# A fused block of four token mixers on one core: other buffer counts, priority bands and assumed latencies around two recurrences

## Chip, cores and metric

One NeuronCore of a Trainium2 chip runs the whole layer in one launch. The metric is the device time of that launch in microseconds; smaller is better. TensorE is called PE here (PEld is its weight load), VectorE DVE, ScalarE ACT, GpSimd POOL and SyncE SP.

## What is computed

For 512 tokens of width 2048 (one batch, float32) the layer normalises x, projects it with `w_in` into five groups, runs four mixers of 1024 channels each, gates the joined result with silu(z) and projects it back with `w_out`:

```python
h = rms_norm(x, norm_g[l])
p = jnp.einsum('bsd,dn->bsn', h, w_in[l])
p_rwkv, p_fox, p_gdn, p_diff, z = jnp.split(p, bounds, axis=-1)
y = jnp.concatenate([rwkv7_time_mix(p_rwkv, ...), forgetting_attention(p_fox, ...),
                     gated_deltanet(p_gdn, ...), differential_attention(p_diff, l, ...)], axis=-1)
x = x + jnp.einsum('bsm,md->bsd', y * jax.nn.silu(z), w_out[l])
```

Two mixers are recurrences over the tokens (`rwkv7_time_mix` with a state of 64 x 64 per head, `gated_deltanet` with 128 x 128 per head, after a causal convolution of 4 taps over its q, k and v); two are softmax attentions.

## The kernel before

Every projection is split into three float32r matmuls (high x high, low x high, high x low). A raw weight tile `wr` of 128 x 1024 comes by one or two DMAs from SP's queue; `wsplit` makes `wh` from it with a cast on ACT (L313) and `wl` with a subtraction on DVE (L314). `wr`, `wh` and `wl` are rings of buffers (`tag`, `bufs`).

`main()` is a stream of projections. After a prologue it runs eight steps `j`, each for one slice of 128 channels of all four mixers: r, k, v of rwkv (`acc_r`, `acc_k`, `acc_v`), then v, k, q of the delta net (`acc_gv`, `acc_gk`, `acc_gq`), then `acc_fqk`, `acc_vv`, `acc_dqk` of the attentions. Then come the z projections (`acc_z`) and the output projection (`acc_o`). The mixers run as threads (Python generators) beside the stream. In step `j` the two recurrences of slice `j-1` and the attention `diff` of `j-1` are still at work: `rwkv_chain` in eight chunks (`pC`), `gdn_chain` in four (`pG`). A chunk of `rwkv_chain` goes PE (`pC<-ZV,ET` and `pC<-Sb,AR`), ACT copy `rs` (L712), DVE addition `rs` (L717), ACT copy `yt` (L719), PE (`pC<-rs,ET`), DVE copy `ZV` (L725), PE (`pC<-ZV,...`), DVE update `Sb`. The chunk of a chain is written chunk c of chain j below.

The order on PE is fixed while the program is built: `pe[0]` adds up an assumed time of the matmuls written so far, a thread that yields a number is taken up again 1.25 times (`SLACK`) that many microseconds later, and between the two the stream writes matmuls. A thread or the stream that yields a name waits until that part has been written. So a yield is an assumed latency: too small a number makes PE meet an instruction whose input is late, too large a number makes a recurrence slow. The order on DVE, ACT, POOL and SP comes from a scheduler that takes priorities: `band(...)` sets them (`PRIO_CHAIN` first, then `PRIO_W`, `PRIO_EVAC`, `PRIO_MIX`, `PRIO_FILL`, `PRIO_GEMM`). On the chip each engine works through its queue strictly as built.

`gdn_evac` (L793) convolves a projection into `gc_v`, `gc_k` or `gc_q`. `gdn_local` applies silu to them, loads and prepares the decay tile `GA` (DMA L821, sixteen operations on POOL at L828, an exponential on ACT at L830), transposes and forms `pK`. `inverses` solves the triangular systems on DVE (`bP`, `bX`, L970) and multiplies their blocks on PE (`pmr`, `pmg`). `put_y` stores a finished slice to DRAM.

Of the kernel before, what the change touches and what calls it, by code (L numbers as in the profile page):

```python
# [20 lines left out]
P = 128  # L21
# [33 lines left out]
def hybrid_kernel(ctx: ExitStack, tc: tile.TileContext, ins, out, steps=tuple(range(NJ)), ydbg=None, tail=True):  # L55
# [71 lines left out]
    def until(*what):  # L127

        while what not in done:
            yield 0.5  # L130
# [85 lines left out]
    for part in range(4):  # L216
        if part == 2:
            load_x(1)
        wr = wp.tile([P, 1024], F32, name=f"w0r{part}", tag="wr", bufs=3) if part < 2 else \
            mp.tile([P, 1024], F32, name=f"w0r{part}")  # L220
        load_tm(wr, part, FOX0 + 2 * G, DIFF0 + 2 * G)
        w0.append((wr, mp.tile([P, 1024], F32R, name=f"w0h{part}"), mp.tile([P, 1024], F32R, name=f"w0l{part}")))
# [92 lines left out]
        return wh, wl  # L315

    def wtile():
        return wp.tile([P, WN], F32, name=f"wr{wcount[0]}", tag="wr", bufs=3)

    def gemm_fm(c0, name, then=None):  # L320
        acc = None
# [44 lines left out]
    ydr = [dr.tile([P, T], F32, name=f"ydr{m}") for m in range(MT)]  # L366

    def put_y(m, y):
        nc.sync.dma_start(ydr[m], y)
        if ydbg is not None:  # L370
            nc.sync.dma_start(ydbg[m], y)

# [321 lines left out]
    def rwkv_chain(j, st, XT):  # L694
# [7 lines left out]
        for c in range(NCH):  # L702
            AR, ET, BKt, ZV = (st[n][c // 4][:, c % 4] for n in ("AR", "ET", "BKt", "ZV"))
            yield from free("cr")
            ps = bank("cr", f"pC{j}_{c}", 1.0e9)

            for h in range(2):
                hs = slice(h * C, (h + 1) * C)
                MM(ps[0:R_, P + h * C:P + (h + 1) * C], ET[:, h, 0:R_], ZV[:, hs], start=True, stop=True)
            if c:  # L710
                MM(ps[:, 0:P], AR.rearrange("p a t -> p (a t)"), Sb, start=True, stop=True)
            nc.scalar.copy(rs[0:C], ps[0:C, P:2 * P])  # L712
            yield 2.4
            y = yt[(c % 2) * C:(c % 2 + 1) * C, c // 2, :]
            if c:
                band(PRIO_CHAIN)
                TT(rs[0:C], rs[0:C], ps[0:C, 0:P], op=ALU.add)  # L717
                band(PRIO_MIX)
                nc.scalar.copy(y, ps[C:P, 0:P])  # L719
            for h in range(2):  # L720
                hs = slice(h * C, (h + 1) * C)
                MM(ps[0:R_, 2 * P + h * C:2 * P + (h + 1) * C], ET[:, h, 0:R_], rs[:, hs], start=True, stop=True)
            yield 2.0
            band(PRIO_CHAIN)
            nc.vector.tensor_copy(ZV[0:C, :], ps[0:C, 2 * P:3 * P])  # L725
            band(PRIO_MIX)
            for h in range(2):
                hs = slice(h * C, (h + 1) * C)
                MM(ps[C:P, 3 * P + h * C:3 * P + (h + 1) * C], ET[:, h, R_:R_ + C], ZV[:, hs], start=True, stop=True)

            if c < NCH - 1:
                for h in range(2):
                    hs = slice(h * C, (h + 1) * C)
                    MM(ps[hs, P:P + C], BKt[:, h], ZV[:, hs], side=2, start=True, stop=True)
            pe[0] += 0.2
            if c < NCH - 1:
                band(PRIO_CHAIN)
                W = Wc[:, c:c + 1]
                tS = mp.tile([P, C], F32, name=f"tS{j}_{c}", tag="tS", bufs=1)
                for h in range(2):  # L740
                    hs = slice(h * C, (h + 1) * C)
                    if c:
                        TS(tS[hs, :], Sb[hs, hs], W[hs, :], None, op0=ALU.mult)
                for h in range(2):
                    hs = slice(h * C, (h + 1) * C)
                    o = ps[hs, P:P + C]
                    if c:
                        STT(Sb[hs, hs], o, W[hs, :], tS[hs, :], op0=ALU.mult, op1=ALU.add)
                    else:
                        TS(Sb[hs, hs], o, W[hs, :], None, op0=ALU.mult)  # L750
                band(PRIO_MIX)
            if c:
                TT(y, y, ps[C:P, 3 * P:4 * P], op=ALU.add)
            else:
                nc.scalar.copy(y, ps[C:P, 3 * P:4 * P])
            release(f"pC{j}_{c}", 3.0)
            if c % 4 == 3:
                done.add(("rwkv_half", j, c // 4))

# [24 lines left out]
    def gdn_evac(j, i, acc):  # L784
        s = "qkv"[i]
        n = 8 * i + j
        if s == "v":
            a = mp.tile([P, T], F32, name=f"gc_{s}{j}", tag="gc_v", bufs=1)
        else:
            a = mp.tile([P, T], F32, name=f"gc_{s}{j}", tag=f"gc_{s}", bufs=1)  # L790
        ACT(a, acc, AF.Copy, scale=convw(3, n))
        for d in (1, 2, 3):
            STT(a[:, d:T], acc[:, 0:T - d], convw(3 - d, n), a[:, d:T], op0=ALU.mult, op1=ALU.add)  # L793
        return a
# [19 lines left out]
        return pt  # L814

    def gdn_local(j, res):

        yield from until("gdn_chain", j - 1)
        GA = mp.tile([P, NT, 2, P], F32, name=f"GA{j}", tag="GA", bufs=1)
        Dm = GA[:, :, 1, :]  # L820
        nc.gpsimd.dma_start(Dm, gcd[:, j, :].unsqueeze(0).to_broadcast([P, NT, P]))  # L821
        gdn_silu(j, "v", res["v"])
        yield 2.5
        band(PRIO_FILL)
        for c in range(NT):
            for b in range(4):
# [5 lines left out]
                                fill=0.0, base=0, channel_multiplier=-1)  # L832
        band(PRIO_MIX)

        yield from until("gk", j)
        k2 = res["k"]
        gdn_silu(j, "k", k2)
        yield 7.0
        yield from free("tr")
        pt = gdn_transposed(j, "k", k2)  # L840
        KTs = mp.tile([P, NT, P], F32, name=f"KTs{j}", tag="KTs", bufs=1)
# [15 lines left out]
        vn = mp.tile([P, NT, P], F32, name=f"vn{j}", tag="vn", bufs=1)  # L857
        TT(vn, pt.rearrange("p (t f) -> p t f", f=P), vn_s.unsqueeze(2).to_broadcast([P, NT, P]), op=ALU.mult)

        yield from until("gq", j)  # L860
        q2 = res["q"]
        gdn_silu(j, "q", q2)
        yield 8.0
        for q in range(2):
            yield from free("sc")
            ps = psc(f"pK{j}_{q}", 2.5)
# [16 lines left out]
    def gdn_chain(j, st, XG):  # L883
# [3 lines left out]
        for c in range(NT):  # L887
# [3 lines left out]
            if c:  # L891
# [2 lines left out]
                rs = mp.tile([P, P], F32, name=f"grs{j}_{c}", tag="gs", bufs=4)  # L894
                band(PRIO_CHAIN)
                STT(rs, ps[:, 0:P], eg_neg[:, c, j:j + 1], vn[:, c, :], op0=ALU.mult, op1=ALU.add)
                band(PRIO_MIX)
                ACT(ot[:, c, :], ps[:, P:2 * P], AF.Copy, scale=eg[:, 0, c, j:j + 1])
            else:
                rs = vn[:, 0, :]  # L900
            yield 2.4
            MM(ps[:, 2 * P:3 * P], XG[:, c, :], rs, start=True, stop=True)
            Y = mp.tile([P, P], F32, name=f"gY{j}_{c}", tag="gs", bufs=4)
            band(PRIO_CHAIN)
            nc.scalar.copy(Y, ps[:, 2 * P:3 * P])
            band(PRIO_MIX)
            yield 2.4
            if c < NT - 1:
                MM(ps[:, 0:P], KTs[:, c, :], Y, start=True, stop=True)
            MM(ps[:, 3 * P:4 * P], GA[:, c, 1, :], Y, start=True, stop=True)  # L910
# [8 lines left out]
            else:  # L919
                TS(ot[:, c, :], ps[:, 3 * P:4 * P], -1.0, None, op0=ALU.mult)  # L920
            band(PRIO_MIX)
            release(f"pG{j}_{c}", 3.2)
        done.add(("gdn_chain", j))
        sq = mp.tile([P, T], F32, name=f"osq{j}", tag="tmp", bufs=2)
        ACT(sq, ot.rearrange("p t f -> p (t f)"), AF.Square)
# [23 lines left out]
    def inverses(j, ET, GA, blk, start_rwkv):  # L949
# [14 lines left out]
        nc.gpsimd.memset(Xf[64:112, 1:512:34], 1.0)  # L964
        pr = lcp.tile([112, 512], F32, name=f"bP{j}", tag="lc", bufs=8)
        for t in range(1, 32):
            band(PRIO_FILL)
            n, w = (t + 1) // 2, t + 1
            pv_ = pr[:, 0:n * w].rearrange("p (a b) -> p a b", b=w)
            TT(pv_, X[:, 0:n, 0:w], A[:, 0:w, t].unsqueeze(1).to_broadcast([112, n, w]), op=ALU.mult)  # L970
# [20 lines left out]
        XQ = mp.tile([P, 4, 32], F32, name=f"XQ{j}", tag="gs", bufs=4)  # L991
        for g in range(4):
            nc.gpsimd.dma_start(XQ[32 * g:32 * g + 32], xb[16 + g:32:4].rearrange("m s t -> s m t"))
        yield 14.5
        yield from until("rwkv_local", j)

        XN = lcp.tile([P, 16, 32], F32, name=f"XN{j}", tag="lc", bufs=8)
# [84 lines left out]
    def qk_heads(j, ev, kind):  # L1082
# [1 line left out]
        gi = 0 if kind == "fox" else 2  # L1084
        TS(ss, ss, 1.0 / C, 1e-6, op0=ALU.mult, op1=ALU.add)
        rs = rsqrt(mp, ss, 16, "qk", f"{kind}{j}")
        yield 3.0
        rv = rs.rearrange("p (t s h) -> p t s h", t=NT, s=2)
        for s, dst in enumerate((qa, ka)):
            dv = dst.rearrange("p t (h f) -> p t h f", f=C)  # L1090
            TT(dv, dv, rv[:, :, s].unsqueeze(3).to_broadcast([P, NT, 2, C]), op=ALU.mult)
        yield 1.2

        parts = []
        for s, src in enumerate((qa, ka)):
# [189 lines left out]
    def main():  # L1285
# [15 lines left out]
        for j in steps:  # L1301
# [21 lines left out]
            for i in (2, 1, 0):  # L1323
                s_ = "qkv"[i]
                acc = yield from gemm_fm(GDN0 + i * G + j * P, f"g{s_}{j}")
                yield "gdn_chain" if i < 2 else "gdn_local", j - 1
                band(PRIO_EVAC)
                gres[s_] = gdn_evac(j, i, acc)
                done.add(("g" + s_, j))
# [164 lines left out]
```

## Time and profile before

| | |
|---|---|
| median of 3 runs | 2264.02 us (2262.28 to 2264.04) |
| the profiled execution | 2263.21 us, of which the span from first to last instruction is 2261.5 us |
| mean granted clock of PE | 0.993 of full speed |
| busy | PE 2209.2 us (98%), DVE 1363.8 us (60%), ACT 804.5 us (36%), POOL 246.7 us (11%) |
| weights and other loads of SP's queue | 187.05 MB |

The span is cut by the profile into work and waits of each engine. PE is busy nearly throughout, so the time can fall only where PE stands idle, where its clock is low, or where it has less to do.

### The profile page before, as it was taken

Reading aid. Unit: us, or ns where it says so; the run is one execution under the profiler, and the core shown is the slowest. Engines: PE = TensorE matmul, PEld = TensorE weight load, DVE = VectorE, ACT = ScalarE, POOL = GpSimd, SP = SyncE. Lnnn points to the kernel's source line nnn. Section 1 sums busy time; section 2 is a strip of 40 time slices with the busy share of each in tenths; the row PEclk is TensorE's granted clock in tenths of the full one; section 3 lists DMA queues with packets and bytes.
Section 4 is the critical chain, followed back from the end, with each engine's and each line's share of the span. In section 5 each row is a group of like instructions: output and inputs, shape, how many; then the busy total and the mean of one; then the engine's idle time right before and its main releaser. Section 6 shows DMA issues by size and latency. Waiting matters only on the chain.

```text
span 2261.5 us, 37256 instructions
## 1 busy us (share of the span) xinstructions
PE 2209.2 (98%) x14604; PEld 1893.5 (84%) x14604; DVE 1363.8 (60%) x3601; ACT 804.5 (36%) x1504; POOL 246.7 (11%) x506
## 2 busy tenths in 40 slices
PE   7999999999999999999999999899999999999999
PEld 6789789879878977987997897798788888888887
DVE  6368588576857957767685695776553434322222
ACT  4233443443353343344335334334422223321121
POOL 2200121112102011110210211111000000100000
PEclk9999999999999999999999999999999999999999
DMA  5433323323322332332332333233346444654443
GB/s 167 104 88 94 97 74 90 97 66 94 98 72 73 93 96 58 94 101 61 85 107 63 80 82 98 65 96 105 96 137 181 119 125 120 163 136 116 113 125 75
DMA packets 321874, 226.33 MB, mean 100 GB/s; under 512 B 17423, under 2 KB 285394, under 8 KB 321186
## 3 DMA queue, kind: packets, MB, share of 16 engines
q1 hardware_dynamic: 298722, 187.05, 31.3%
q0 software_dynamic: 9152, 15.37, 3.2%
q10 hardware_dynamic: 13824, 21.54, 2.9%
q8 instruction: 115, 1.88, 0.3%
q14 instruction: 61, 0.50, 0.1%
HBM read 203.93 MB, written 19.97 MB: 99 GB/s over the span
## 4 chain that ended last, share of the span: by engine, by line
PE 90%; DVE 5%; POOL 2%; DMA 1%; ACT 1%; issue 1%; SPq 0%; ACTq 0%; DVEq 0%
PE acc_z L70 16%; PE acc_o L70 15%; PE acc_dqk L70 8%; PE acc_fqk L70 8%; PE acc_vv L70 6%; PE acc_k L70 4%; PE acc_v L70 4%; PE acc_r L70 4%; PE acc_gv L70 4%; PE acc_gk L70 4%; PE pC L70 3%; POOL GA L828 2%; PE acc_gq L70 2%; PE pG L70 1%; PE pSf L70 1%; DMA GA<-gcd 1%
## 5 line engine op out<-in xcount | busy, mean ns | idle before, releaser
L314 DVE TENSOR_TENSOR wl<-wr,wh 128x1024 fp32r<-128x1024 f32 x318 | 389.0, 1224 | 534.5 <-ACT wh L313 527.7
L313 ACT CAST wh<-wr 128x1024 fp32r<-128x1024 f32 x318 | 333.9, 1050 | 750.8 <-PE acc_o L70 231.8
L70 PE MATMUL acc_z<-hh,wh 128*128 128x512 f32 x512 | 204.5, 399 | 0.0
L70 PE MATMUL acc_z<-hh,wl 128*128 128x512 f32 x512 | 199.7, 390 | 0.0
L70 PE MATMUL acc_z<-hl,wh 128*128 128x512 f32 x512 | 199.6, 390 | 0.0
L70 PE MATMUL acc_o<-wh,gl 128*128 128x512 f32 x512 | 183.6, 389 | 0.0
L70 PE MATMUL acc_o<-wl,gh 128*128 128x512 f32 x512 | 177.6, 389 | 0.0
L70 PE MATMUL acc_o<-wh,gh 128*128 128x512 f32 x512 | 176.2, 389 | 0.0
L70 PE MATMUL acc_fqk<-wh,hh 128*128 128x256 f32 x512 | 151.8, 296 | 0.8 <-DVE gssk L807 0.8
L70 PE MATMUL acc_fqk<-wl,hh 128*128 128x256 f32 x512 | 145.1, 283 | 0.0
L70 PE MATMUL acc_fqk<-wh,hl 128*128 128x256 f32 x512 | 144.9, 283 | 0.0
L70 PE MATMUL acc_dqk<-wh,hh 128*128 128x256 f32 x512 | 138.2, 292 | 0.0
L970 DVE TENSOR_TENSOR bP<-bX,bA 112x2 f32<-112x2 f32 (+30 forms) x248 | 122.1, 492 | 24.1 <-POOL bA L958 18.5
L70 PE MATMUL acc_dqk<-wh,hl 128*128 128x256 f32 x512 | 133.6, 283 | 0.0
L70 PE MATMUL acc_vv<-wh,hh 128*128 128x256 f32 x448 | 120.4, 290 | 0.0
L70 PE MATMUL acc_vv<-wh,hl 128*128 128x256 f32 x448 | 116.9, 282 | 0.0
L70 PEld LDWEIGHTS acc_z<-hh,wl 128*128 128x128 f32 x512 | 96.1, 188 | 20.5
L70 PEld LDWEIGHTS acc_o<-wl,gh 128*128 128x128 f32 x512 | 96.1, 188 | 20.2 <-DVE wl L314 0.3
L70 PEld LDWEIGHTS acc_o<-wh,gl 128*128 128x128 f32 x512 | 96.1, 188 | 20.0
L70 PEld LDWEIGHTS acc_o<-wh,gh 128*128 128x128 f32 x512 | 96.0, 188 | 20.1 <-ACT wh L313 0.2
L70 PEld LDWEIGHTS acc_z<-hh,wh 128*128 128x128 f32 x512 | 96.2, 188 | 19.4 <-issue 0.7
L70 PEld LDWEIGHTS acc_z<-hl,wh 128*128 128x128 f32 x512 | 96.3, 188 | 18.4
(515 smaller groups left out, 5226.4 us busy)
## 6 DMA issues: line engine op xcount, KB each, us to landing
wr<-in_w_in SPq DMA_DIRECT2D x162, 512.0 KB
wr<-in_w_in SPq DMA_DIRECT2D x184, 256.0 KB
wr<-in_w_out SPq DMA_DIRECT2D x64, 512.0 KB
zy<-ydr ACTq DMA_DIRECT2D x30, 256.0 KB
nb<-cdr SPq DMA_DIRECT2D x8, 512.0 KB
xo<-in_x ACTq DMA_DIRECT2D x16, 256.0 KB
gr<-gdr POOLq DMA_DIRECT2D x16, 256.0 KB, 5.1
out<-xo ACTq DMA_DIRECT2D x16, 256.0 KB
```

What stands on the lines that cost most here:

```text
L70: return nc.tensor.matmul(o, a, b, **kw)
L313: nc.scalar.copy(wh[:, 0:n], wr[:, 0:n])
L314: TT(wl[:, 0:n], wr[:, 0:n], wh[:, 0:n].bitcast(F32), op=ALU.subtract)
L828: nc.gpsimd.tensor_scalar(Dm[:, c, bs], Dm[:, c, bs], gcx[:, b, c * 8 + j:c * 8 + j + 1], 0.0, op0=ALU.subtract, op1=ALU.min)
L970: TT(pv_, X[:, 0:n, 0:w], A[:, 0:w, t].unsqueeze(1).to_broadcast([112, n, w]), op=ALU.mult)
```

## The change

The buffers of `gc_k` and `gc_q` become two, and the stream waits at k and q of step `j` for the delta net's chain of `j-2` in place of `j-1`. `wr` has two buffers in place of three. `put_y` goes from SP's queue to POOL's. In `gdn_local` the three silu come first, and only then the wait for the chain of `j-1` and the load of `GA`; one yield of 8 becomes 4, one of 7 falls away. The copy `yt` of `rwkv_chain` and the scaled copy `vn` of `gdn_chain` move from `PRIO_MIX` to `PRIO_CHAIN`, the solve from `PRIO_FILL` to `PRIO_MIX`. The yields of both chains become smaller, two yields of `qk_heads` larger, one of `inverses` smaller. No matmul is added or taken away.

```diff
-        wr = wp.tile([P, 1024], F32, name=f"w0r{part}", tag="wr", bufs=3) if part < 2 else \
+        wr = wp.tile([P, 1024], F32, name=f"w0r{part}", tag="wr", bufs=2) if part < 2 else \
...
-        return wp.tile([P, WN], F32, name=f"wr{wcount[0]}", tag="wr", bufs=3)
+        return wp.tile([P, WN], F32, name=f"wr{wcount[0]}", tag="wr", bufs=2)
...
-        nc.sync.dma_start(ydr[m], y)
+        nc.gpsimd.dma_start(ydr[m], y)
...
             nc.scalar.copy(rs[0:C], ps[0:C, P:2 * P])
-            yield 2.4
+            yield 1.8
             y = yt[(c % 2) * C:(c % 2 + 1) * C, c // 2, :]
             if c:
                 band(PRIO_CHAIN)
                 TT(rs[0:C], rs[0:C], ps[0:C, 0:P], op=ALU.add)
+                nc.scalar.copy(y, ps[C:P, 0:P])
                 band(PRIO_MIX)
-                nc.scalar.copy(y, ps[C:P, 0:P])
...
-            yield 2.0
+            yield 1.5
             band(PRIO_CHAIN)
             nc.vector.tensor_copy(ZV[0:C, :], ps[0:C, 2 * P:3 * P])
...
-            release(f"pC{j}_{c}", 3.0)
+            release(f"pC{j}_{c}", 2.4)
...
-            a = mp.tile([P, T], F32, name=f"gc_{s}{j}", tag=f"gc_{s}", bufs=1)
+            a = mp.tile([P, T], F32, name=f"gc_{s}{j}", tag=f"gc_{s}", bufs=2)
...
     def gdn_local(j, res):
+        gdn_silu(j, "v", res["v"])
+        yield 2.5
+        yield from until("gk", j)
+        k2 = res["k"]
+        gdn_silu(j, "k", k2)
+        yield 2.5
+        yield from until("gq", j)
+        q2 = res["q"]
+        gdn_silu(j, "q", q2)
+        yield 2.5
 
         yield from until("gdn_chain", j - 1)
         GA = mp.tile([P, NT, 2, P], F32, name=f"GA{j}", tag="GA", bufs=1)
...
-        gdn_silu(j, "v", res["v"])
-        yield 2.5
...
-        yield from until("gk", j)
-        k2 = res["k"]
-        gdn_silu(j, "k", k2)
-        yield 7.0
...
-        yield from until("gq", j)
-        q2 = res["q"]
-        gdn_silu(j, "q", q2)
-        yield 8.0
+        yield 4.0
...
                 STT(rs, ps[:, 0:P], eg_neg[:, c, j:j + 1], vn[:, c, :], op0=ALU.mult, op1=ALU.add)
+                ACT(ot[:, c, :], ps[:, P:2 * P], AF.Copy, scale=eg[:, 0, c, j:j + 1])
                 band(PRIO_MIX)
-                ACT(ot[:, c, :], ps[:, P:2 * P], AF.Copy, scale=eg[:, 0, c, j:j + 1])
...
-            yield 2.4
+            yield 2.0
...
-            yield 2.4
+            yield 1.8
...
-            release(f"pG{j}_{c}", 3.2)
+            release(f"pG{j}_{c}", 2.6)
...
         for t in range(1, 32):
-            band(PRIO_FILL)
+            band(PRIO_MIX)
...
-        yield 14.5
+        yield 12.5
...
         rs = rsqrt(mp, ss, 16, "qk", f"{kind}{j}")
-        yield 3.0
+        yield 4.0
...
-        yield 1.2
+        yield 2.0
...
                 acc = yield from gemm_fm(GDN0 + i * G + j * P, f"g{s_}{j}")
-                yield "gdn_chain" if i < 2 else "gdn_local", j - 1
+                yield ("gdn_chain", max(j - 2, steps[0] - 1)) if i < 2 else ("gdn_local", j - 1)
```

What this does to the queues is seen at three places. Names carry the slice `j` and the chunk, then a running number.

PE in step 3 at chunk 4 of chain 2, before. `pG2_3` is the last chunk of the delta net's chain 2, `pB3_0` transposes for slice 3, `acc_gq3` is the q projection of step 3:

```order
L70 MATMUL pA3_0_1_7475<-AR3_0_7450,BK3_7228 128x128
L70 MATMUL pC2_4_7494<-ZV2_1_6225,ET2_1_5888 66x64 x2
L70 MATMUL pC2_4_7494<-Sb2_6992,AR2_1_5832 128x128
L70 MATMUL pG2_3_7453<-grs2_3_7456,GA2_5398 128x128
L74 MATMUL pB3_0_7503<-ident_72,BK3_7228 128x128 x4
L70 MATMUL pC2_4_7494<-rs2_6994,ET2_1_5888 66x64 x2
L70 MATMUL pG2_3_7453<-gY2_3_7500,GA2_5398 128x128
L70 MATMUL acc_gq3_7550<-hh_79,wh84_7546 128x512
```

PE in step 3 at the end of `acc_gk3`, now. `pd2` belongs to the attention of slice 2:

```order
L70 MATMUL pC2_6_7549<-ZV2_1_5762,ET2_1_5587 66x64 x2
L70 MATMUL pC2_6_7549<-Sb2_6892,AR2_1_5541 128x128
L70 MATMUL acc_gk3_7359<-hh_79,wh83_7462 128x512
L70 MATMUL acc_gk3_7359<-hl_80,wh83_7462 128x512
L70 MATMUL acc_gk3_7359<-hh_79,wl84_7463 128x512
L70 MATMUL acc_gq3_7570<-hh_79,wh84_7566 128x512
L70 MATMUL acc_gq3_7570<-hl_80,wh84_7566 128x512
L70 MATMUL acc_gq3_7570<-hh_79,wl85_7567 128x512
L74 MATMUL pB3_0_7574<-ident_72,BK3_7329 128x128 x4
L70 MATMUL pd2_7105<-V2_5956,prd2_3_0_7377 128x128 x4
L70 MATMUL pC2_6_7549<-rs2_6894,ET2_1_5587 66x64 x2
L70 MATMUL acc_gq3_7570<-hh_79,wh84_7566 128x512
```

Before, no projection matmul stands between `pC<-Sb,AR` and `pC<-rs,ET` of this chunk, since the stream waits for chain 2 of the delta net there; now the projections go on through the place, and the rwkv chain is two chunks further.

DVE at the same chunk, before. `ET3_0` are eight masked products for slice 3, `gc_k3` the convolution of k:

```order
L896 SCALAR_TENSOR_TENSOR grs2_3_7456<-pG2_3_7453,eg_neg_600,vn2_5700 128x128
L743 TENSOR_SCALAR tS2_4_7573<-Sb2_6992,Wc2_5088 64x64 x2
L793 SCALAR_TENSOR_TENSOR gc_k3_7539<-acc_gk3_7288,vec2_583,gc_k3_7539 128x511
L1220 TENSOR_REDUCE dso2_7467<-dsq2_7463 128x4
L793 SCALAR_TENSOR_TENSOR gc_k3_7539<-acc_gk3_7288,vec2_583,gc_k3_7539 128x510
L646 SCALAR_TENSOR_TENSOR ET3_0_7472<-pA3_0_0_7474,NV3_7362,mask2_522 128x2x64 x4
L646 SCALAR_TENSOR_TENSOR ET3_0_7472<-pA3_0_1_7475,NV3_7362,mask2_522 128x2x64 x2
L1221 TENSOR_TENSOR dso2_7467<-dso2_7467,s0_2_7084 128x4
L646 SCALAR_TENSOR_TENSOR ET3_0_7472<-pA3_0_1_7475,NV3_7362,mask2_522 128x2x64 x2
L717 TENSOR_TENSOR rs2_6994<-rs2_6994,pC2_4_7494 64x128
L793 SCALAR_TENSOR_TENSOR gc_k3_7539<-acc_gk3_7288,vec2_583,gc_k3_7539 128x509
L665 TENSOR_TENSOR BKt3_0_7502<-pB3_0_7503,NV3_7362 128x512
```

DVE around the addition `rs` at the end of `acc_gk3`, now:

```order
L935 TENSOR_TENSOR rsy_go2_7469<-rsy_go2_7469,gsc2_5656 128x4
L936 TENSOR_TENSOR vn2_5812<-vn2_5812,rsy_go2_7469 128x512
L717 TENSOR_TENSOR rs2_6894<-rs2_6894,pC2_6_7549 64x128
L314 TENSOR_TENSOR wl86_7652<-wr85_7649,wh85_7651 128x1024
L665 TENSOR_TENSOR BKt3_0_7545<-pB3_0_7574,NV3_7421 128x512
L793 SCALAR_TENSOR_TENSOR gc_k3_7559<-acc_gk3_7359,vec2_583,gc_k3_7559 128x511
L725 COPY ZV2_1_5762<-pC2_6_7549 64x128
```

Before, two convolution steps and all of `ET3_0` stand ahead of `rs` of chunk 4; now the convolution stands behind `rs` of chunk 6. In chain 4 (and 1), however, `ET` now stands ahead of the copy `ZV` of chunk 5. DVE there, now (`rsq_go`, `rsy_go` are steps of a reciprocal square root, `prd4` belongs to the attention):

```order
L1204 SCALAR_TENSOR_TENSOR prd4_3_0_11749<-prd4_3_1_11754,smd4_3_1_11755,prd4_3_0_11749 128x512
L160 TENSOR_TENSOR rsq_go4_11769<-rsy_go4_11768 128x4
L161 TENSOR_TENSOR rsq_go4_11769<-rsq_go4_11769,rsh_go4_11770 128x4
L162 SCALAR_TENSOR_TENSOR rsy_go4_11768<-rsq_go4_11769,rsy_go4_11768 128x4
L160 TENSOR_TENSOR rsq_go4_11769<-rsy_go4_11768 128x4
L314 TENSOR_TENSOR wl133_11907<-wr132_11904,wh132_11906 128x1024
L161 TENSOR_TENSOR rsq_go4_11769<-rsq_go4_11769,rsh_go4_11770 128x4
L646 SCALAR_TENSOR_TENSOR ET5_0_11809<-pA5_0_0_11811,NV5_11734,mask2_522 128x2x64 x4
L646 SCALAR_TENSOR_TENSOR ET5_0_11809<-pA5_0_1_11812,NV5_11734,mask2_522 128x2x64 x3
L725 COPY ZV4_1_10172<-pC4_5_11790 64x128
```

Between `rs` and this `ZV` stand in all eleven small operations, one of 128 x 512, one `wl` and seven of `ET`. PE has three `pd` and six `acc_gk` matmuls between the two.

ACT around the exponential of `GA3`, before:

```order
L313 CAST wh86_7684<-wr86_7681 128x1024
L712 COPY rs2_6994<-pC2_5_7639 64x128
L830 ACTIVATE GA3_7554<-GA3_7554 128x4x128
L719 COPY yt2_6991<-pC2_5_7639 64x128
L1234 ACTIVATE yd2_7661<-pdo2_7656,sub8_588 128x512
```

ACT around the exponential of `GA3`, now (its line is L838, that of the copy `yt` L718):

```order
L718 COPY yt2_6891<-pC2_5_7440 64x128
L313 CAST wh84_7566<-wr84_7564 128x1024
L838 ACTIVATE GA3_7778<-GA3_7778 128x4x128
L1146 COPY prd2_3_0_7377<-pPd2_3_7539 128x512
L712 COPY rs2_6894<-pC2_6_7549 64x128
L313 CAST wh85_7651<-wr85_7649 128x1024
L791 ACTIVATE gc_k3_7559<-acc_gk3_7359,vec2_583 128x512
L718 COPY yt2_6891<-pC2_6_7549 64x128
```

Before, the copy `yt` of chunk 5 stands behind the exponential; now it stands ahead of it, and the copies `rs` and `yt` of chunk 6 behind it, with a cast and an evacuation between them.

## Rows read from the trace of the kernel before

**Rows 1.** Busy time by engine, seven stretches of 190 us from 230 to 1560: their sum.
```profile
sum 1330.00, PE 1298.66 PEld 1134.59 DVE 957.63 ACT 536.94 POOL 198.69; mean PE 185.52 PEld 162.08 DVE 136.81 ACT 76.71 POOL 28.38
```
**Rows 2.** Waits of PE: instruction waiting, releaser, us in total, times, longest.
```profile
PE pC L70 <- ACT yt L719: 20.0, 7, 3.4
PE ptfox L74 <- DVE qafox L1091: 6.1, 6, 1.1
PE pgk L74 <- ACT yd L1234: 2.0, 2, 1.6
PE pG L70 <- ACT vn L898: 1.4, 1, 1.4
```
**Rows 3.** Timeline 680.5 to 691: start us, us, engine, line, instruction, idle before.
```profile
681.86 0.44 PE L70 MATMUL pC<-Sb,AR 128*128 128x128 f32 x2
682.34 0.26 ACT L712 COPY rs<-pC 64x128 f32<-64x128 f32 x1 [0.41 <-PE pC L70]
682.98 0.74 DVE L793 SCALAR_TENSOR_TENSOR gc_k<-acc_gk,vec,gc_k 128x510 f32<-128x510 f32 x1
683.64 1.63 DVE L646 SCALAR_TENSOR_TENSOR ET<-pA,NV,mask 128x128 f32<-128x128 f32 x6
685.77 0.27 DVE L717 TENSOR_TENSOR rs<-rs,pC 64x128 f32<-64x128 f32 x1
686.08 0.26 ACT L719 COPY yt<-pC 64x128 f32<-64x128 f32 x1 [3.25 <-DVE rs L717]
686.39 0.71 PE L70 MATMUL pC<-rs,ET 128*66 128x64 f32 x4 [3.44 <-ACT yt L719]
```
**Rows 4.** Two stretches of 50 us: busy us by engine, then granted clock, DMA share, GB/s.
```profile
650.00:700.00 50.00, 46.56 (x287) 37.73 (x286) 40.42 (x131) 20.81 (x47) 11.27 (x23) 0.93 0.23 54
...
1450.00:1500.00 50.00, 47.73 (x378) 44.89 (x377) 32.47 (x108) 15.52 (x28) 11.40 (x25) 0.97 0.28 77
```
**Rows 5.** Timeline 1445 to 1461 of PE, POOL and ACT.
```profile
1445.56 0.44 PE L70 MATMUL pG<-gY,GA 128*128 128x128 f32 x2
...
1446.30 0.79 POOL L821 DMA_DIRECT2D GA<-gcd  x1
1451.67 7.59 POOL L828 TENSOR_SCALAR GA<-GA,gcx 128x32 f32<-128x32 f32 x16 [4.59 <-DMA GA<-gcd]
...
1459.29 0.63 ACT L830 ACTIVATE GA<-GA 128x512 f32<-128x512 f32 x1 [4.91 <-POOL GA L828]
...
1460.26 0.54 PE L70 MATMUL pC<-rs,ET 128*66 128x64 f32 x4 [2.27 <-ACT yt L719]
```
**Rows 6.** Timeline of DVE, 929 to 931: small operations of three interleaved chains.
```profile
929.94 0.17 DVE L160 TENSOR_TENSOR rsq_qkfox<-rsy_qkfox 128x16 f32<-128x16 f32 x1
930.02 0.16 DVE L161 TENSOR_TENSOR rsq_gn<-rsq_gn,rsh_gn 128x8 f32<-128x8 f32 x1
```
**Rows 7.** Timeline 1403 to 1409: one chunk of the recurrence without a wait.
```profile
1404.85 0.26 ACT L719 COPY yt<-pC 64x128 f32<-64x128 f32 x1 [0.34 <-DVE rs L717]
...
1408.31 0.40 PE L70 MATMUL pC<-rs,ET 128*66 128x64 f32 x4
```
**Rows 8.** The page's queue row, a DMA issue row, and timelines from 1700 to 1713.
```profile
q1 hardware_dynamic: 298722, 187.05, 31.3%
...
blk<-GA POOLq DMA_DIRECT2D x32, 16.0 KB, 1.7
...
1702.90 1.23 DVE L314 TENSOR_TENSOR wl<-wr,wh 128x1024 fp32r<-128x1024 f32 x1 [4.06 <-ACT wh L313]
...
1707.31 1.05 ACT L313 CAST wh<-wr 128x1024 fp32r<-128x1024 f32 x1 [3.95 <-PE acc_z L70]
1712.74 1.05 ACT L313 CAST wh<-wr 128x1024 fp32r<-128x1024 f32 x1 [4.38 <-PE acc_z L70]
```
**Rows 9.** Timeline 794 to 817 of DVE and PE: from the solve's result to its matmuls.
```profile
798.87 0.76 DVE L999 STREAM_TRANSPOSE XN<-ET 32x256 f32<-32x256 f32 x2
...
814.73 0.45 PE L70 MATMUL pmr<-XN,ET 32*32 32x32 f32 x32
```

## Prediction

> **What bounds the kernel.** I began with the busy time by stretches. In the seven stretches of a whole step each, PE is busy 1298.66 of 1330.00 us, DVE 957.63 [rows 1]. PE is the bound there, and its idle time, 31.3 us, is nearly all that an edit which adds and removes no matmul can win in these steps. So I next read the waits of PE: which instruction waits, and whose result ends the wait. Four rows carry 29.5 us: `pC` for the copy `yt` of ACT 20.0, `ptfox` for DVE 6.1, `pgk` for the ACT operation `yd` 2.0, `pG` for `vn` 1.4 [rows 2]. All four belong to what the change touches. Last, the granted clock in stretches of 50 us, because an idle PE may cost more than the idle time: it is 1.00 but for a stretch at 0.93 and four at 0.97, those that hold or follow the longest of these waits [rows 4].
>
> The largest row is one event told five times. In chains 2 to 6 at chunk 4 PE waits 3.44 us for `rs` and `yt` [rows 3]; the five come to 17.2. The timeline shows why. The copy `rs` of ACT is done at 682.60. The addition `rs` on DVE could follow, but ahead of it in DVE's queue stand convolution steps of `gc_k` (0.74) and eight `ET` (six of them 1.63, so 0.27 each); it starts at 685.77. The idle time is on PE because the stream itself waits at that place for the chain of the delta net, so that no projection matmul stands between. The other 2.8 of the row are a second event, once for certain: ACT takes the exponential of `GA` first, which waits 4.91 for POOL's sixteen operations, and `yt` stands behind it; PE waits 2.27 [rows 5].
>
> **What the change removes.** The five waits of 17.2: with two buffers of `gc_k` and `gc_q` the stream goes on at that place, and in the new order the convolution and `ET` are no longer ahead of `rs` of chunk 4. The 2.8 behind the exponential: `yt` is now written in the higher band and stands ahead of it. `ptfox`, 6.1 in six waits of 1.1 at most: its two yields grow by 1.0 and 0.8, times 1.25 is 2.25 us later, twice the longest wait. `pgk`, 2.0: `yd` was behind the same exponential. `pG`, 1.4: `vn` is now in the chains' band. Together 29.5.
>
> **The clock.** One stretch of 50 us at 0.93 and four at 0.97 cost 50 x (0.07 + 4 x 0.03) = 9.5 us of matmul time [rows 4]. The waits before them were the 3.44 and 2.27; smaller ones left the clock at 1.00. If no long wait is left, all returns; if new ones of 2 us appear, part stays. I take half, 4.75; bounds 0 and 9.5.
>
> **What the change adds on the path.** The yields of the rwkv chain fall from 2.4, 2.0 and 3.0 to 1.8, 1.5 and 2.4; times 1.25, PE meets `rs` 0.75 us, `ZV` 0.62 us and `Sb` 0.75 us sooner. A chunk without a wait has `yt` ready at 1405.11 and its matmul starts at 1408.31, so 3.2 us to spare [rows 7]; others have less, down to none. Most chunks stay covered by that; four places do not, and I price each by what stands in the new queues, with durations from the rows: a projection matmul of 512 columns 5.43 / 24 = 0.226, `wl` 1.23, a cast 1.05 [rows 8], a `pG` matmul 0.44 / 2 = 0.22, a small `pC` one 0.54 / 4 = 0.135 and a 128 x 512 of ACT 0.63 [rows 5], a 128 x 512 of DVE 0.74 and an `ET` 0.27 [rows 3], a small DVE operation about 0.12, since of 0.17 long ones the next starts after 0.08 [rows 6].
>
> First, `ZV` of chunk 5 in chains 1 and 4. On DVE eleven small operations 1.3, one of 128 x 512 0.74, a `wl` 1.23 and seven `ET` 1.9 make 5.2. On PE six projection matmuls 1.36, three `pd` 0.66 and the `pC` 0.5 make 2.5. DVE is 2.7 later, less what was to spare: 3.2 - 0.75 = 2.45 at best, nothing at worst. So 0.3 to 2.7; the middle, 1.4, for each: 2.8.
>
> Second, `rs` of chunk 3 in chains 0, 3 and 6. Between `rs` of chunk 2 and this one my sum over DVE's new queue is 11.3, over PE's 10.9 (33 projection matmuls 7.5, ten more of 256 or 512 columns 1.6, the rest `pC` and `pG`). So the little that is to spare is used up and not earned again. 0 to 2.7 as before; I take 1.1 each: 3.3.
>
> Third, `rs` and `yt` of chunk 6 behind the exponential. It ends 13.9 us after the last `pG` matmul of the delta net (1446.0 to 1459.92 [rows 5]), a time that the change leaves as it is: DMA, POOL, exponential. In chains 2 and 5 ACT then still has the copy of `pPd` 0.63, `rs` 0.26, a cast 1.05, the first step of `gc_k` 0.63 and `yt` 0.26: 16.7. PE reaches the place after 39 projection matmuls 8.8, seven `pd` and two others of 128 x 128 2.0, and 29 small ones 3.9: 14.7. So 2.0 each, 4.0. In chains 0, 3 and 6 ACT has two of 0.63, a cast, the step of `gc_k`, `rs` and `yt`, 17.4, and PE 48 projection matmuls and the like, 16.3: 1.1 each, 3.3. In chains 1 and 4 PE comes at 18.7, and nothing waits. Bounds 0, if ACT's queue runs closer than I add it up, and 7.5.
>
> Fourth, the chunks of the delta net, with yields 0.5 to 0.75 us shorter: 0 to 0.5 in each of seven chains, 0 taken. The sum of new waits is 2.8 + 3.3 + 7.3 = 13.4; by the bounds 0 to 5.4 + 8.1 + 7.5 + 3.5 = 24.5.
>
> **What is costed at nothing.** Two weight buffers in place of three: the queue moved 187.05 MB in 31.3% of 2261.5 us, so a tile of 0.524 MB occupies the engines 2.0 us, and the shortest landing shown is 1.7 [rows 8]: 3.7 is my estimate of a load alone. With two buffers the load for the next but one cast can start when `wl` is done, 1704.13, and the cast reads it at 1712.74: 8.6 us, 4.9 to spare. `put_y` on POOL: SP's queue then carries loads only, and what POOL issues behind a waiting `put_y` are the solve's DMAs. The solve's last transpose ends at 799.63 and PE uses it at 814.73 [rows 9]: 15 us hide some eight issues of 0.8 and the yield of `inverses` that is 2.5 us shorter. The solve's higher band puts its operations ahead of others on DVE; it runs in the prologue of a chain, and the queue sums above have it in them.
>
> **The sum.** The profiled execution took 2263.21; less 29.5, less 4.75, plus 13.4 is 2242.4. The median of the runs stands 0.8 above this execution: 2243.
>
> **Rivals.** (A) As summed: 2243.
>
> (B) The waits only move. DVE and ACT are busy no less than before, and the budgets are smaller: if the new waits in the chains grow to the 20.0 + 2.0 + 1.4 = 23.4 removed there and the clock stays as it is, only `ptfox` is won, 2264 - 6.1 = 2258. For it speaks that the third place is worked out to a wait of 2.0, as long as the old one of 2.27; against it, that the 3.44 had an emptied PE queue as its cause, which is gone.
>
> (C) DVE's queue is slower than my sums: if each operation starts only when the one before has ended, the eleven small ones cost 0.17 each, the eight-step chains between them gaps on top, and the leads of all chunks melt. With 5 us of new waits in each of the seven chains, 35: 2263.2 - 29.5 + 35 + 0.8 = 2269.5, slower. It decides from 30 us of new waits on, 4.3 a chain. Against it: operations of 0.17 and 0.16 start 0.08 apart [rows 6]. The Trainium skill, "VectorE: DVE Perf Modes", section "The DRAIN you can't avoid", has this rule: the next operation does not start until the pipeline of the one before is empty; the same section sends the reader to an exception for operations that are not held. By the rule the time would be that of C; here the trace disagrees for these operations, with 0.08 measured.
>
> (D) Two weight buffers are too few in the stretches of `acc_z` and `acc_o`, where casts follow every 5.43 us [rows 8]. It decides when a load takes over 8.6 us from its issue; half a microsecond late on some 100 tiles gives 50 us: 2243 + 50 = 2293. With two buffers the load has no second period in reserve, and the profile of before shows no such load.
>
> (E) No effect: the removed waits were sheltering others, and new ones take exactly their place: 2262.
>
> **Numbers.** A 0.68, B 0.16, E 0.07, C 0.06, D 0.03. Low: all of the clock, and only the new waits of the third place in chains 2 and 5: 2263.2 - 29.5 - 9.5 + 4.0 + 0.8 = 2229; 2228. High: the upper bound of new waits and no clock is 2263.2 - 29.5 + 24.5 + 0.8 = 2259; the range reaches on to E, 2262. Left out are C, D and the tails of A and E. A measurement here tells 0.2%, 4.5 us, from no change, so faster is below 2259.5: A and two thirds of B, 0.79; the same is the rest of B and most of E, 0.12; slower is C, D, 0.09.
>
> **What would show it.** In the waits of PE of the changed kernel the row of `pC` for `yt` falls from 20.0 to some 7 to 14 and no wait of 3.44 stands at chunk 4; `ptfox`, `pgk` and `pG` are gone or under 1. The longest waits left stand at `rs` of chunk 6 in chains 2 and 5, some 2 us, ended by ACT, and at `ZV` of chunk 5 in chains 1 and 4, ended by DVE. The seven stretches have PE busy above 1310 of 1330 us for the same work, and the clock is 1.00 but for a stretch or two. Casts that wait for a DMA in `acc_z` would show D; DVE's queue always later than PE at `rs` would show C. I would be wrong if the stream, free to run on at k, meets another wait for the chain of the delta net at `gdn_local`, which the changed `until` puts later in the step.

## The result, and the profile after

The changed kernel takes 2239.7 us (median of 4 runs, 2238.13 to 2241.18); the kernel before, in the same comparison, 2263.15. The ratio is 0.9897, its 95% interval 0.988 to 0.9914: faster by 1%. The forecast was 2243, range 2228 to 2262. The profiled execution took 2240.12, its span is 2238.4.

The span is shorter by 23.1 us. PE's busy time fell from 2209.2 to 2198.9, by 10.3, for the same matmuls; its idle time (span less busy) from 52.3 to 39.5, by 12.8. The four largest rows of PE's waits in the changed kernel, without those of the prologue, columns as in [rows 2]:

```profile
PE pC L70 <- ACT yt L718: 9.8, 10, 1.5
PE pC L70 <- DVE ZV L725: 2.6, 2, 1.3
PE acc_vv L70 <- ACT kafox L1077: 2.6, 3, 0.9
PE pmg L70 <- DVE XNg L1004: 1.6, 1, 1.6
```

All four rows of [rows 2], 29.5 us, are gone in their old form; the first row here has the old name but other places. New waits of 16.6 us, the sum of the four rows shown, stand against them. The clock, in the two stretches of [rows 4] and in the one that still shows a dip (columns as there):

```profile
600.00:650.00 50.00, 48.41 (x383) 38.19 (x380) 22.42 (x65) 19.79 (x50) 8.44 (x17) 0.97 0.33 89
650.00:700.00 50.00, 49.54 (x321) 39.46 (x320) 45.00 (x133) 25.30 (x55) 11.04 (x27) 1.00 0.26 63
...
1450.00:1500.00 50.00, 49.15 (x419) 48.39 (x418) 38.77 (x135) 16.86 (x26) 6.11 (x11) 1.00 0.34 90
```

Between 100 and 2200 us only the first is below 1.00; it holds the wait of `pmg`, 1.6 us. The stretches with the other new waits, 1.5 us at most, show 1.00.

The timeline at chunk 4 of chain 2, the place of [rows 3]: `rs` of DVE starts 1.31 us after ACT's copy has ended, where it was 3.17, and PE does not wait.

```profile
667.00 0.26 ACT L712 COPY rs<-pC 64x128 f32<-64x128 f32 x1
668.57 0.27 DVE L717 TENSOR_TENSOR rs<-rs,pC 64x128 f32<-64x128 f32 x1
668.87 0.26 ACT L718 COPY yt<-pC 64x128 f32<-64x128 f32 x1
669.56 0.40 PE L70 MATMUL pC<-rs,ET 128*66 128x64 f32 x4
```

The timeline at two of the places that the prediction priced: `ZV` of chunk 5 in chain 1, where `wl` and seven `ET` stand ahead of it, and `rs` of chunk 3 in chain 3 behind a `wl`.

```profile
494.63 1.27 DVE L314 TENSOR_TENSOR wl<-wr,wh 128x1024 fp32r<-128x1024 f32 x1
495.90 1.89 DVE L646 SCALAR_TENSOR_TENSOR ET<-pA,NV,mask 128x128 f32<-128x128 f32 x7
497.72 0.27 DVE L725 COPY ZV<-pC 64x128 f32<-64x128 f32 x1
498.04 0.27 PE L70 MATMUL pC<-ZV,ET 128*64 128x64 f32 x1 [1.28 <-DVE ZV L725]
...
846.49 1.21 DVE L314 TENSOR_TENSOR wl<-wr,wh 128x1024 fp32r<-128x1024 f32 x1
847.63 0.27 DVE L717 TENSOR_TENSOR rs<-rs,pC 64x128 f32<-64x128 f32 x1
847.93 0.26 ACT L718 COPY yt<-pC 64x128 f32<-64x128 f32 x1 [0.68 <-DVE rs L717]
848.25 0.45 PE L70 MATMUL pC<-rs,ET 128*66 128x64 f32 x4 [1.37 <-ACT yt L718]
```

### The profile page after: what moved, and what is told of

Its sections match the earlier page's. It is cut to its first block, busy times and chain, and to the rows that moved or that the text cites. A ratio compares the mean times of both kernels' runs of the same rounds, so it can differ in the third digit from the quotient of the medians.

```text
span 2238.4 us, 37383 instructions
## 1 busy us (share of the span) xinstructions
PE 2198.9 (98%) x14604; PEld 1888.7 (84%) x14604; DVE 1372.6 (61%) x3601; ACT 800.1 (36%) x1504; POOL 262.5 (12%) x538
## 4 chain that ended last, share of the span: by engine, by line
PE 89%; DVE 4%; DMA 3%; ACT 2%; POOL 1%; issue 1%; SPq 0%; ACTq 0%; DVEq 0%; POOLq 0%
PE acc_z L70 16%; PE acc_o L70 15%; PE acc_fqk L70 8%; PE acc_dqk L70 8%; PE acc_vv L70 7%; PE acc_k L70 4%; PE acc_v L70 4%; PE acc_gq L70 4%; PE pC L70 3%; PE acc_r L70 3%; PE acc_gv L70 3%; PE acc_gk L70 3%; POOL GA L836 1%; PE pG L70 1%; PE pSf L70 1%; DVE wl L314 1%
## 5 line engine op out<-in xcount | busy, mean ns | idle before, releaser
L70 PEld LDWEIGHTS acc_z<-hh,wh 128*128 128x128 f32 x512 | 96.2, 188 | 19.5 <-issue 0.4
```

Of the source, the lines that this page charges most:

```text
L70: return nc.tensor.matmul(o, a, b, **kw)
```

## The experiments

Two sums, both made from the built programs, set the expectations. A **planned stop** is a jump of `pe[0]` while the stream waits for a name: for that long the plan has no matmul to write. They add up to 22.8 planned us before, all for the delta net's chain (about 4.2 in each of the chains 2 to 6, those with a wait of 3.44, and the rest in chain 1), and to 0 in the changed kernel; these are assumed times, not measured ones. The **queue sums** add the work on DVE and on PE between one operation of the rwkv chain and the next, with durations of the trace before; where DVE's is longer, beyond what was to spare, PE should wait. They gave 3.6 us at chunk 4 in chains 2 to 6 of the kernel before, where 3.44 were measured.

**One buffer again.** All five engines have the same instructions in the same order as in the changed kernel.

```diff
-            a = mp.tile([P, T], F32, name=f"gc_{s}{j}", tag=f"gc_{s}", bufs=2)
+            a = mp.tile([P, T], F32, name=f"gc_{s}{j}", tag=f"gc_{s}", bufs=1)
...
-                yield ("gdn_chain", max(j - 2, steps[0] - 1)) if i < 2 else ("gdn_local", j - 1)
+                yield "gdn_chain" if i < 2 else "gdn_local", j - 1
```

> The changed kernel with one buffer of gc_k and gc_q again and the stream's old wait for the delta net's chain at k and q. The instructions of all five engines come out in the same rows as in the changed kernel; only tiles share memory again. Theory of the prediction (the second buffer is what removed the five waits of 3.44 us): the five waits come back, 17 us and some of the clock, 2255 to 2263. Rival (with the smaller yields the delta net's chain has been written before the stream reaches k, so the wait and the buffer bind nothing): 2238 to 2242, as the changed kernel, and no wait of 3.44 us.

Measured 2239.76 (ratio to before 0.9891, 95% interval 0.9876 to 0.9906; the numbers in brackets below are the same two), row of `pC` for `yt` 10.0, longest 1.6. The rival holds: beside the other edits the second buffer gives nothing.

**Only the second buffer.** Kernel before with the two edits above the other way round, and `wr` with `bufs=2`.

> The kernel before with only the second buffers of gc_k and gc_q, the stream's later wait, and two weight tiles (three do not fit beside them). If the stream's stop at k alone makes the five waits: 2263 - 17.2 - 5 to 8 of clock = 2238 to 2241, with the row of ptfox (6.1) still there. If the waits only move, as DVE's queue is unchanged in length: 2255 to 2263. If two weight tiles are too few: over 2265, with casts that wait for a DMA.

Measured 2258.23 (0.9973, 0.9962 to 0.9983). The row of `pC` for `yt` falls from 20.0 to 0.7, and what replaces it before the end of the last step are single waits of 2.0 us at most: the first theory was right about the place. But the time comes back where the steps end. The longest new row of PE's waits:

```profile
PE ptdiff L74 <- DVE Qldiff L1104: 5.0, 2, 3.7
```

Two stretches at the end of the last step, columns as in [rows 4]:

```profile
1500.00:1550.00 50.00, 38.78 (x247) 30.47 (x246) 42.98 (x152) 19.50 (x44) 6.14 (x12) 0.86 0.29 80
1550.00:1600.00 50.00, 41.75 (x309) 33.35 (x308) 28.03 (x68) 15.62 (x37) 8.34 (x15) 0.90 0.29 79
```

PE is idle 11.2 and 8.3, 19.5 of 100 us, and the clock falls to 0.86 and 0.90. The stream ran ahead of the recurrences, and then had to stop for the last slice: the plan has stops of 33.4 us for `solved` and 4.9 for `inverses`. In this run the stop that was taken away is paid at the end.

**Both chains' yields back.** Changed kernel, both sets of yields as before.

```diff
-            yield 1.8
+            yield 2.4
...
-            yield 1.5
+            yield 2.0
...
-            release(f"pC{j}_{c}", 2.4)
+            release(f"pC{j}_{c}", 3.0)
```

(and 2.0, 1.8, 2.6 of `gdn_chain` to 2.4, 2.4, 3.2)

> The changed kernel with the yields of both chains as before (2.4, 2.0, 3.0 and 2.4, 2.4, 3.2). If the new waits of pC (9.8 for yt, 2.6 for ZV) come from the smaller yields: most of the 12.4 goes, 2228 to 2234. If ACT's exponential makes them whatever the yields: 2236 to 2240. If the longer chains hold the stream up at another place: 2242 to 2255.

Measured 2237.17 (0.988, 0.9865 to 0.9895), above the first expectation and within the second. The row of `ZV` goes, that of `yt` falls only to 7.6, of which 3.2 are one wait behind an exponential that waits 4.74 for POOL:

```profile
701.90 0.63 ACT L838 ACTIVATE GA<-GA 128x512 f32<-128x512 f32 x1 [4.74 <-POOL GA L836]
702.55 0.26 ACT L718 COPY yt<-pC 64x128 f32<-64x128 f32 x1
```

The waits at chunk 4 of the chains 2 to 6 do not come back, though the yields are the old ones. Nor is the bill of the run with the buffers alone paid: from 1500 to 1600 us PE stands idle 1.3 us, not 19.5.

**Yields of `qk_heads` back.** Changed kernel, 4.0 to 3.0 and 2.0 to 1.2.

> The changed kernel with the two yields of qk_heads as before (3.0 and 1.2). If these alone removed the wait of ptfox (6.1 in six): it comes back, 2244 to 2248. If the order of DVE's queue removed it: no change, 2238 to 2242.

Measured 2240.06 (0.9895, 0.9879 to 0.9912), and no row of `ptfox`: its own yields are not what removes it here. Other rows shift (`pC` 11.4, `pG` for `vn` 5.1, `kafox` 0.9).

**Only the three rwkv yields.** Kernel before, with the three lines of the diff above the other way round.

> The kernel before with one edit: the three yields of rwkv_chain of the changed kernel (1.8, 1.5, 2.4). While the program is built, the stream then never has to stop for the delta net's chain; in the kernel before these stops add up to 22.8 planned us. If those stops are the cause of the five waits: 2236 to 2246, with ptfox (6.1) still there. If the second buffer or the other edits are needed as well: 2255 to 2264.

Measured 2225.29 (0.9831, 0.9817 to 0.9846), 11 us below the lower end of the expectation: three numbers give more than the whole change. The two longest rows of PE's waits outside the prologue:

```profile
PE pC L70 <- ACT yt L719: 5.7, 3, 2.9
PE pPf L74 <- ACT prf L1145: 2.4, 2, 1.4
```

And the timeline at one of these three waits, 2.61 us, where the exponential stands in front of `yt`:

```profile
505.78 0.63 ACT L830 ACTIVATE GA<-GA 128x512 f32<-128x512 f32 x1 [4.10 <-POOL GA L828]
506.44 0.26 ACT L719 COPY yt<-pC 64x128 f32<-64x128 f32 x1
506.75 0.45 PE L70 MATMUL pC<-rs,ET 128*66 128x64 f32 x4 [2.61 <-ACT yt L719]
```

The rows of `ptfox`, `pgk` and `pG` in [rows 2] are gone, and that of `pC` is down from 20.0 to 5.7, with no edit to bands, `qk_heads` or buffers. That `ptfox` would stay was expected and did not come true; why it goes was not found.

**First two rwkv yields back**, third at 2.4, one buffer (changed kernel, 1.8 to 2.4 and 1.5 to 2.0).

> The changed kernel with one buffer of gc_k and gc_q, and the first two rwkv yields as before (2.4 and 2.0; the third stays 2.4). No stop of the stream is planned, and the sums of DVE's and PE's queues give no wait for DVE. Theory (new waits come from DVE's queue against PE's, and these can be read from the two sums): the 2.6 of ZV and half of the 9.8 of yt go, 2230 to 2236. If the waits come from ACT's exponential: 2236 to 2241.

Measured 2227.93 (0.9841, 0.9825 to 0.9857). The row of `ZV` is gone, that of `yt` 5.9, and no other row of PE's waits in the steps is over 0.3. The time lies 2 us below the expected range, and 11.8 below the run with one buffer alone (2239.76): beside the other edits the smaller first two yields cost time.

**An earlier load of `GA`.** As the last, with `bufs=2` for `GA` and its load and POOL's operations moved to the start of `gdn_local`.

> As the run with the first two rwkv yields back, and GA has two buffers: its load and POOL's sixteen operations stand at the start of gdn_local, a quarter of a step earlier, and only the exponential at the old place. Theory (ACT stands at the exponential waiting for POOL, and yt behind it): the waits of pC for yt nearly all go, 2224 to 2232. If the exponential costs nothing by now: as without it, 2230 to 2236.

Measured 2229.16 (0.9848, 0.9833 to 0.9862). The edit did not do what it was made for: POOL's DMA of `GA` still waits 23.7 us for `pG` in six steps (26.0 in seven without it), and the exponential waits as long for POOL as without it (4.10 at 1055.13, for 4.15 at 1052.63). What holds the load was not found; the run says nothing on the exponential.

**A collision on purpose.** Changed kernel, one buffer, rwkv yields 2.1, 1.8, 2.4.

> The changed kernel with one buffer of gc_k and gc_q and the rwkv yields 2.1, 1.8, 2.4, between the old and the new. No stop of the stream is planned either, but in DVE's new queue the convolution or the masked products stand ahead of rs of chunk 4, and the two sums give a wait of 3.3 in chains 1 to 5 and 2.2 in chain 6, 19.7 in all. Theory (a wait is where DVE's queue is longer than PE's): 2250 to 2262. If only the planned stops of the stream matter: 2230 to 2240.

Measured 2269.11 (1.0022, 1.0012 to 1.0031), 7 us above the expected range and slower than before, with no planned stop: that the plan has none is not enough. The row of PE's waits:

```profile
PE pC L70 <- ACT yt L718: 24.0, 8, 4.1
```

The timeline at chunk 4 of chain 2:

```profile
670.52 1.22 DVE L314 TENSOR_TENSOR wl<-wr,wh 128x1024 fp32r<-128x1024 f32 x1
671.65 0.74 DVE L607 SCALAR_TENSOR_TENSOR ta<-rw_r,vec,ta 128x512 f32<-128x512 f32 x1
672.32 0.74 DVE L793 SCALAR_TENSOR_TENSOR gc_v<-acc_gv,vec,gc_v 128x511 f32<-128x511 f32 x1
...
673.58 0.68 DVE L1133 CUSTOM_DVE_ANT_0 prd<-pSd,al 128x512 f32<-128x512 f32 x1
674.19 0.28 DVE L717 TENSOR_TENSOR rs<-rs,pC 64x128 f32<-64x128 f32 x1
675.13 0.61 ACT L1193 ACTIVATE al<-al 128x512 f32<-128x512 f32 x1
675.76 0.26 ACT L718 COPY yt<-pC 64x128 f32<-64x128 f32 x1
676.08 0.45 PE L70 MATMUL pC<-rs,ET 128*66 128x64 f32 x4 [3.83 <-ACT yt L718]
```

One of the stretches of 50 us that hold such a wait:

```profile
850.00:900.00 50.00, 45.92 (x270) 37.31 (x269) 39.43 (x121) 20.11 (x41) 12.35 (x28) 0.90 0.24 60
```

Ahead of `rs` on DVE stand a `wl`, a product `ta` of the next slice of rwkv, one convolution step (of `gc_v`) and two `prd` of the attention, and none of the masked products that the expectation named; then `yt` starts 1.3 us after `rs` has ended, behind ACT's work for the attention. The sum of 19.7 was right in place and too small: the six waits at chunk 4 of the chains 1 to 6 come to 22.5.

**Only the yield of `inverses`.** Kernel before, 14.5 to 12.5.

> The kernel before with one edit: the yield of inverses is 12.5 in place of 14.5, so both recurrences of a step start 2.5 planned us sooner. The planned stops of the stream fall from 22.8 to 5.8 us, and the queue sums give 1.2 us of waits for DVE. Theory (the stops set the five waits): about three quarters of the gain that the three rwkv yields gave alone, 2231 to 2244. If any stop at all brings the whole wait of 3.44 back: 2255 to 2262.

Measured 2246.13 (0.992, 0.9906 to 0.9935), 2 us above the expectation: the row of `pC` falls from 20.0 to 4.6, but `ptfox` stays, at 6.9, and rows of 3.2 and 2.9 for `vn` and `wl` come up. With stops of 22.8, 5.8 and 0 planned us the kernel before thus stands at 2264, 2246 and 2225.

**Both chains' yields alone.** Kernel before, six yields of the change.

> The kernel before with the yields of both chains of the changed kernel. No stop is planned, as with the rwkv yields alone; the queue sums give 5.1 us of waits for DVE against 2.2 there. Theory (the delta net's smaller yields win nothing more and bring waits): 2226 to 2234, not faster than 2225.3. If the delta net's chain is what holds the stream up: 2215 to 2223.

Measured 2231.41 (0.9856, 0.9842 to 0.9871), 6 us over the rwkv yields alone. The new row is `pd` waiting for the ACT copy `prd`, 6.3 in six; `prd` stands directly behind the exponential, which waits 5.4 to 7.0 us for POOL.

**Copies back.** Changed kernel, `yt` and `vn` in the band of before.

> The changed kernel with the copies yt and vn in the band of before. The rows of PE, DVE, POOL and SP stay as in the changed kernel; only ACT's order differs, and yt of chunk 6 stands behind the step of gc_k in chains 2 and 5. If the bands alone kept yt ahead of the exponential and won the 2.8 and 1.4 of the prediction: 2242 to 2247. If the chains merely reach the exponential at another chunk: 2238 to 2242.

Measured 2239.36 (0.989, 0.9873 to 0.9906), rows of `pC` 10.4 and 2.6. The program built with this edit is the changed kernel, instruction for instruction: against the expectation ACT's order does not differ, and in both `yt` of chunk 6 in chain 2 stands behind the step of `gc_k`. So the two bands do nothing in the changed kernel, and the run repeats it: 10.4 for 9.8 is what such a row moves by itself.

**Three edits together.** Kernel before with the rwkv yields, `inverses` at 12.5 and `yt` in the chains' band.

> The kernel before with the three rwkv yields, the yield of inverses 12.5, and yt in the chains' band; nothing else. No stop is planned and the queue sums give no wait for DVE in any chain. Of the 2225.3 of the rwkv yields alone the waits of 2.9 in chain 0 (DVE) and 2.6 in chain 1 (yt behind the exponential) should go: 2217 to 2222. If the chains, now sooner, meet other work of ACT: 2223 to 2230.

Measured 2226.42 (0.9834, 0.9819 to 0.9848), not told apart from 2225.29. The queue sums gave no wait; the chip shows 7.5 us in six. One of them on the timeline:

```profile
499.74 0.63 ACT L830 ACTIVATE GA<-GA 128x512 f32<-128x512 f32 x1 [4.96 <-POOL GA L828]
500.27 1.03 ACT L313 CAST wh<-wr 128x1024 fp32r<-128x1024 f32 x1
501.34 1.28 DVE L314 TENSOR_TENSOR wl<-wr,wh 128x1024 fp32r<-128x1024 f32 x1 [1.66 <-ACT wh L313]
502.73 0.75 DVE L793 SCALAR_TENSOR_TENSOR gc_k<-acc_gk,vec,gc_k 128x511 f32<-128x511 f32 x1
505.42 0.63 ACT L799 ACTIVATE gt_k<-gc_k 128x512 f32<-128x512 f32 x1 [2.68 <-DVE gc_k L793]
506.18 0.27 DVE L717 TENSOR_TENSOR rs<-rs,pC 64x128 f32<-64x128 f32 x1
507.33 0.45 PE L70 MATMUL pC<-rs,ET 128*66 128x64 f32 x4 [2.11 <-ACT yt L718]
```

The late exponential makes the cast late, the cast `wl`, and behind `wl` stand the convolution and `rs`. ACT's step `gt_k` waits for that convolution, and it and a further cast stand ahead of `yt`. A sum over one queue alone does not see a wait that comes over from another engine.

## Why the prediction was right, and where it was not

The total came out within 0.2%, and the signs of all large terms were right; the reason given for the largest was not. That it came so close is in part luck: the clock gave back 5.5 us more than was taken, and the new waits cost 3.2 more.

- **The five waits of 17.2: right in size and place, not in what they depend on.** The step "with two buffers of `gc_k` and `gc_q` the stream goes on at that place" names an edit that the changed kernel does not need: with one buffer it runs the same instructions in the same order, in the same time. What the runs without the waits have in common is a plan that stops little or not at all for the delta net's chain (the collision shows that this alone is not enough), and several edits do that by themselves: the rwkv yields (stops from 22.8 to 0), the yield of `inverses` (to 5.8), and the buffers, which however lose most of the gain at the end of the steps. None of the edits that were taken out of the changed kernel brought the waits back, so there the credit cannot be given to one of them. The third rwkv yield, the yield of `inverses`, the new order in `gdn_local` and the solve's band were not taken out one by one.
- **The 2.8 behind the exponential, `ptfox` and the two small rows: gone, for other reasons than given.** The bands of `yt` and `vn`, credited with 2.8 and 1.4, change no instruction of the changed kernel. With its own yields back `ptfox`, 6.1, stays gone; `pgk`, 2.0, `pG`, 1.4, and `ptfox` go with the three rwkv yields alone. The rwkv chain now meets these places at other chunks.
- **The clock: mis-sized.** 4.75 was taken, half of 9.5; PE's busy time fell by 10.3, and by 12.0 and 13.1 in the two runs with the same order of instructions (one buffer, copies back): the upper bound of 9.5 and a little more. The new waits of 1.5 us at most stand in stretches of 1.00. The forecast's reading left out the first 100 us, which stand at 0.97 before and at 0.97 and 0.93 now; the change does not touch them.
- **New waits: 13.4 forecast, 16.6 measured.** `ZV` of chunk 5 in chains 1 and 4: 1.3 each for 1.4. `rs` of chunk 3 in chains 0, 3 and 6: 1.37 each for 1.1. Chunk 6 in chains 0, 3 and 6: 1.3 to 1.5 each for 1.1. In chains 2 and 5 it is 0.42 for 2.0, and not, as forecast, the longest left, as the rows below show: the exponential ended 13.0 us after the last `pG` matmul (676.37 to 689.39) and not 13.9, since POOL's sixteen operations took 6.64 for 7.59 in [rows 5]; PE came 0.5 later than summed, at 691.6, and ACT's five pieces took 2.6 for 2.8. Not foreseen were `kafox`, 2.6 in three, `pmg`, 1.6, and 0.37 each at chunk 4 of chains 1 and 4.

The timeline of the changed kernel around the exponential in chain 2, and at the wait of `kafox` in step 1, where ACT's square `sqfox` waits for `gssq` of DVE:

```profile
366.81 0.60 ACT L1075 ACTIVATE sqfox<-acc_fqk 128x512 f32<-128x512 f32 x1 [1.39 <-DVE gssq L806]
...
368.00 0.39 PE L70 MATMUL acc_vv<-wh,hh 128*128 128x256 f32 x1 [0.86 <-ACT kafox L1077]
...
675.90 0.47 PE L70 MATMUL pG<-gY,GA 128*128 128x128 f32 x2
...
682.09 6.64 POOL L836 TENSOR_SCALAR GA<-GA,gcx 128x32 f32<-128x32 f32 x16 [4.64 <-DMA GA<-gcd]
...
688.76 0.63 ACT L838 ACTIVATE GA<-GA 128x512 f32<-128x512 f32 x1 [7.04 <-POOL GA L836]
...
691.71 0.26 ACT L718 COPY yt<-pC 64x128 f32<-64x128 f32 x1
...
692.02 0.45 PE L70 MATMUL pC<-rs,ET 128*66 128x64 f32 x4 [0.42 <-ACT yt L718]
```

- **Costed at nothing.** The 15 us that were to hide the solve's part are not there: in the changed kernel `pmr` comes 1.7 to 7.4 us after the last `XN`, and PE waits 1.6 once. Two weight tiles cost little: no cast in `acc_z` waits for its weights, but two casts of the output projection do (7.0 us, PE not held up), and once PE waits 0.9 for a cast in `acc_o`; all runs with two tiles show 0.7 to 1.0 there, those with three 0.2 at most. Of `put_y` on POOL no row of PE's waits shows a cost.
- **Rivals.** Rival B, "the waits only move" (2258), has the time of the buffers alone, 2258.23, though there they move to the end of the steps and not within the chains. C (a slow DVE queue) and D (too few weight buffers) did not appear, and no stop of the stream at `gdn_local` did.
- **The rest of the change** costs: the whole is 14 us slower than three of its numbers alone. On the kernel before, the delta net's three yields cost 6 of these, with waits behind the exponential. In the changed kernel it is the first two rwkv yields that cost: with these back, and one buffer, it stands at 2227.93. So the same numbers that win alone lose 12 us beside the other edits; which of these they meet was not taken apart.

## What to carry to other kernels

Where a program's order is fixed from assumed latencies, look first for the places at which the plan itself has nothing to write, and make the slow thread end sooner there; a buffer alone, which only let the fast thread run on, deferred the bill to the end. Change such a yield together with a sum over each queue that the next operation stands in: such sums found the places of the waits, though not those that come over from another engine. A pair of values between two better ones (2.1 and 1.8 between 1.8, 1.5 and 2.4, 2.0) was the slowest of all. And before a gain is put down to an edit, take that edit out, and put it in alone: here the most visible one did nothing beside the others, and the bands of two copies did not even change the program.

## What the hardware showed unexpectedly

What a wait cost beyond itself did not go by its length alone. PE and its clock in stretches of 2 us (columns as in [rows 4]): in the kernel before after the wait of 3.44 in chain 2, around the same wait in chain 6, which ends at 1445.27, and after the one of 2.27 behind it; in the changed kernel after the 1.59 of `pmg`; in the run with the rwkv yields alone after the 2.61 shown above.

```profile
688.00:690.00 2.00, 2.00 (x6) 1.52 (x5) 1.91 (x9) 1.76 (x3) 0.72 (x1) 0.50 0.26 43
...
1443.00:1445.00 2.00, 0.00 (x0) 0.00 (x0) 2.00 (x10) 0.04 (x1) 0.00 (x0) 1.00 0.02 6
1445.00:1447.00 2.00, 1.73 (x12) 1.51 (x13) 2.00 (x8) 0.47 (x2) 1.89 (x3) 1.00 0.22 33
...
1461.00:1463.00 2.00, 2.00 (x8) 1.71 (x8) 0.31 (x2) 1.20 (x2) 0.00 (x0) 0.50 0.34 131
...
618.00:620.00 2.00, 2.00 (x8) 1.56 (x7) 0.00 (x0) 0.00 (x0) 0.00 (x0) 0.50 0.93 250
...
508.00:510.00 2.00, 2.00 (x15) 1.42 (x14) 2.00 (x6) 0.36 (x1) 0.00 (x0) 1.00 0.00 1
```

0.50 is the lower of the two levels, 1.2 of 2.4 GHz. The wait of 3.44 was followed by it in chains 2 to 5 and not in chain 6; a wait of 1.59 was, and one of 2.61 was not. What decides it these runs do not show. In sum it is still the long waits that cost: PE's busy time for the same matmuls ran from 2192.0 us (rwkv yields alone, mean clock 0.997) to 2214.3 (the collision, 0.988): 22 us on top of the waits, of which the clock explains some 20 (0.009 x 2214).
